# Pre-norms issued per token tile inside the part before, and first products by token tile, in a two-model transformer kernel on one core

## The chip, the cores and the metric

The kernel runs as one program on one core of a Trainium2 chip. The metric is the device time of one execution in microseconds (us); lower is better. A profiled execution gives, besides its time, a span (from the first to the last instruction) and a record of every instruction on the engines: TensorE (PE; PEld is its weight load), VectorE (DVE), ScalarE (ACT), GpSimd (POOL) and SyncE (SP), which issues the transfers.

## The reference

Two blocks run one behind the other on 256 tokens of width 1024, in float32. Every part is "add the normed output to the residual stream", and every part begins with a norm of that stream (the pre-norm).

```python
# first block
f = swiglu(rmsnorm(h, ffn1_pre_g)); h = h + 0.5 * rmsnorm(f, ffn1_post_g)
z = rmsnorm(h, mix_pre_g) @ w_in          # attention heads and a bidirectional RWKV-7 recurrence
h = h + rmsnorm(concat(y_att, y_rwkv) @ w_out, mix_post_g)
f = swiglu(rmsnorm(h, ffn2_pre_g)); h = h + 0.5 * rmsnorm(f, ffn2_post_g)
# second block, two layers; hc is a second stream of 256 context tokens
hx = rmsnorm(h, norm1_g) * (1 + scale) + shift   # shift, scale from a modulation of c
h = h + gate * mix(hx, hc)                # window attention and an mLSTM
h = h + gate * channel_mix(...)           # layer 0 a swiglu of 2816, layer 1 eight experts
```

swiglu(t) is (silu(t @ w_gate) * (t @ w_up)) @ w_down, with an inner width of 2816 (22 blocks of 128).

## The kernel before, in words

**Tiling.** The stream `hx` lies with tokens on the partitions, as two token tiles of 128 x 1024. A product needs the normed stream transposed (features on the partitions), so a pre-norm is: square with a sum on ScalarE (L184, in `rms_rstd`), `rstd` by two GpSimd instructions (L110, L111, in `rsqrt`), `xn` on VectorE (L217 with a gain row, L215 without), eight 128 x 128 transposes per tile on TensorE (L230 in `norm_rows_T`, L240 in `to_T`), and a split of the result in two float32r halves: `xhi` on ScalarE (L192, L200) and `xlo` on VectorE (L193, L201). Where a scale and a shift are columns (`ada_T`), VectorE applies them behind the transpose (L199).

**Products.** Every float32 product is three float32r products, hi*hi, hi*lo and lo*hi (`mm3`, L160 to L162). Weights are loaded in pieces of 1 MB into three raw buffers (L133) and split as they come, in tiles of 128 x 1024 elements: `whi` on ScalarE (L149), `wlo` on VectorE (L150). A phase has a number of split buffers (`nsplit`); phases lie one over the other in memory, so a buffer of a new phase waits for the last reader of what lay there.

**Parts.** `ffn_block` runs a feed-forward in two halves of 11 blocks of 128 inner features. For each pair of blocks `ffn` multiplies the weights by all 256 tokens, gate and up (192 products of 256 columns for the first four blocks), applies silu and the product (`hh`, already transposed as the down product needs it), and splits it (L276, L277). The down product goes by 512 output columns; the last 512 are done token tile by token tile (L288 to L296), and behind each tile `add_post` does the post-norm (L184, L327) and adds to `hx` (L328). `mix1` is the first mixer: pre-norm, one block of `rwkv_in` (L789), q, k and v of the attention (`mm_N`, token tile by token tile), the heads with the other blocks of `rwkv_in` between them, the recurrence, and `w_out` (L797 to L810), where four accumulators (two tiles, two halves of columns) fill together. `mix2` is the mixer of the second block; its first products take the context tiles first.

**Order.** The program is traced in the order written; the build's scheduler then sets the order on each engine's queue, taking what is ready in its own estimate, earlier-written work first. Each engine then works its queue in that order. Pre-norms stand at the beginning of their part: `norm_rows_T` at L333 and L786, `ada_T` at L881.

Of the kernel before, what the change touches and what calls it, by code (L numbers as in the profile page):

```python
# [9 lines left out]
F32 = mybir.dt.float32  # L10
# [23 lines left out]
class Builder:  # L34
# [185 lines left out]
    def norm_rows_T(self, pool, h, name, bufs=1, tags=("ps",)):  # L220

        x = self.new_xT()
        xn = self.norm_N(h, self.row(pool, name, bufs))
        for t in range(2):
            ts = slice(t * 128, (t + 1) * 128)
            for k0 in range(0, KT, 4):
                p = self.psum(4, 128, tag=tags[(2 * t + k0 // 4) % len(tags)])
                for k in range(4):
                    c = (k0 + k) * 128
                    self.nc.tensor.transpose(p[:, k], xn[t][:, c:c + 128], self.ident)  # L230
                self.split_t((x[0][:, k0:k0 + 4, ts], x[1][:, k0:k0 + 4, ts]), p)
        return x

    def to_T(self, xn, dst, k0, n, g=None, b=None, tag="ps"):
        for kk in range(0, n, 2):
# [14 lines left out]
    def ffn(self, xs, wg, wu, wd, fp, nhalf=2):  # L250
# [3 lines left out]
        for hf in range(nhalf):  # L254
            hhi = fp.tile([128, per, ng * S], F32R, name="hhi")
            hlo = fp.tile([128, per, ng * S], F32R, name="hlo")
            d0 = hf * per
            for blk in range(0, per, 2):
                nb = min(2, per - blk)
                c0 = (d0 + blk) * 128  # L260
                g = self.wsplit(kview(wg, 0, KT, c0, nb * 128), KT, nb * 128)
                u = self.wsplit(kview(wu, 0, KT, c0, nb * 128), KT, nb * 128)
                for j in range(nb):
                    cs = slice(j * 128, (j + 1) * 128)
                    for gi, x in enumerate(xs):
# [13 lines left out]
                yield None  # L279
# [50 lines left out]
    def ffn_block(self, h, pre, wg, wu, wd, post, early=None):  # L330
        nc = self.nc
        with self.phase("fp", 8, gu=2, ps=6) as fp:
            x = self.norm_rows_T(fp, h, pre, 2)  # L333
            if early:
                early()
            grow = self.row(fp, post, 2)
            y = self.row_tiles()
            for r in self.ffn([x], self.I[wg], self.I[wu], self.I[wd], fp):
                if r is not None:
                    hf, c, t, p = r  # L340
                    yv = y[t][:, c * 512:(c + 1) * 512]
                    if hf == 0:
                        nc.scalar.copy(yv, p)
                    else:
                        nc.vector.tensor_tensor(yv, p, yv, op=OP.add)
                        if c == 1:
                            self.add_post(h[:, t], y[t], grow, 0.5)
                yield

# [428 lines left out]
    def mix1(self, side):  # L778
        nc = self.nc
        I = self.I  # L780
        with self.phase("ra") as ra:
            rkv = ra.tile([128, 12, S], F32, name="rkv")
            R = (rkv,) + tuple(ra.tile([128, S], F32, name=n) for n in ("wd", "ad", "gd"))
            R += (ra.tile([128, 4, 2, 2], F32, name="rn"), self.load_const(ra, "k_blk", nc.sync))
            with self.phase("ap", 4, acc=2, rn=1, **{"as": 2}, at=1, av=1, ps=1) as mp:
                x = self.norm_rows_T(mp, self.hx, "mix_pre_g", 1, ("as", "at", "av", "ps"))  # L786
                yT = self.new_xT()
                win = self.rwkv_in(mp, x, R)
                next(win)  # L789
                yield from self.attn1(mp, x, yT, win)  # L790
                yield from win
            with self.phase("rp", None, c0=2, c1=2, c2=2, md=2) as mp:
# [4 lines left out]
                with self.phase("wo", 4) as me:  # L797
                    y = self.row_tiles()
                    grow = self.row(me, "mix_post_g")
                    accs = [[self.psum(512, tag=g) for _ in range(2)] for g in ("md", "c2")]  # L800
                    for kb in range(0, KT, 2):
                        for c in range(2):
                            w = self.wsplit(kview(I["w_out"], kb * 128, 2, c * 512, 512), 2, 512)
                            for t, x, ts in self.tiles((0, yT)):
                                for k in range(kb, kb + 2):
                                    self.mm3(accs[c][t], (x[0][:, k, ts], x[1][:, k, ts]), w(k - kb), k == 0, k == KT - 1)
                    for t in range(2):
                        for c in range(2):
                            nc.scalar.copy(y[t][:, c * 512:c * 512 + 512], accs[c][t])
                        self.add_post(self.hx[:, t], y[t], grow)  # L810
                        yield

# [58 lines left out]
    def mix2(self, L, side, pre=None):  # L871
# [1 line left out]
        w = self.I["w_in_2"][L]  # L873
        both = L == 0
        with self.phase("m2", 4, acc=2, ps=1, at=3, ml=2) as mp:
            if pre is None:
                x = self.ada_T(self.hx, L, 0, 0)
                c = self.ada_T(self.hc, L, 0, 1)
            else:
                c = pre  # L880
                x = self.ada_T(self.hx, L, 0, 0)  # L881
# [30 lines left out]
            first = cx + xx if pre else xx + cx  # L912

            def c_kv(col, n, t, p):
                nc.vector.tensor_tensor(gt[:, t], p[:, 256:272], bg, op=OP.add)
# [571 lines left out]
        yield  # L1487


class Halves:  # L1490


# [141 lines left out]
def program(tc, I, out):  # L1634
    b = Builder(tc, I)
    b.out = out
    with ExitStack() as ctx:
        b.open_pools(ctx)
        b.consts()
        b.cond()  # L1640
        run(b.ffn_block(b.hx, "ffn1_pre_g", "ffn1_w_gate", "ffn1_w_up", "ffn1_w_down", "ffn1_post_g"))
        side = b.mod(0)
        run(b.mix1(side))
        run(side)
        pre = []

        def early():
            b.load_ctx()
            pre.append(b.ada_T(b.hc, 0, 0, 1))

        run(b.ffn_block(b.hx, "ffn2_pre_g", "ffn2_w_gate", "ffn2_w_up", "ffn2_w_down", "ffn2_post_g", early))
# [42 lines left out]
```

## Time and profile before

| | us |
|---|---|
| median of 3 runs | 2451.85 (2451.59 to 2456.05) |
| the profiled execution | 2451.68 |
| its span | 2449.9 |
| TensorE busy | 2346.6 (96%) |
| first feed-forward, about | 0 to 203 |
| first mixer, about | 203 to 538 |
| second feed-forward, about | 538 to 743 |
| second block, about | 743 to 2450 |

The page gives shares for the whole span; the four borders between parts are a small share of it and have to be looked at one by one, by the waits of TensorE, by windows of time, and by the timeline. The granted clock of TensorE has two levels here, 1.00 (2.4 GHz) and 0.50 (1.2 GHz); a mean in between is a stretch with both.

### The profile page before, as it was taken

The page shows a single profiled execution, that of the slowest core. Times are in us where ns is not written, and L with a number is a line of the kernel's source. Part 1 is how long each engine was busy: PE and PEld are TensorE (multiplying, and loading weights), DVE is VectorE, ACT ScalarE, POOL GpSimd, SP SyncE. Part 2 cuts the span into 40 slices and gives each one's busy share as a digit, 9 for nine tenths or more (in the row PEclk, how much of TensorE's full clock was granted, in tenths as well). Part 3 has the DMA queues.
Part 4 walks back from the last instruction along what each step waited for, and adds up shares of the span by engine and source line. Part 5 has one row for each costly group of instructions (what it writes and reads, how often), then busy time and mean ns, then how long its engine had stood idle before and what let it go on. Part 6 is the DMA issues. An engine that isn't in the chain of part 4 may idle for free. (4 is left out here: it accounts for less than half of the span.)

```text
span 2449.9 us, 38791 instructions
## 1 busy us (share of the span) xinstructions
PE 2346.6 (96%) x15592; PEld 1963.8 (80%) x15592; DVE 1614.4 (66%) x2427; ACT 1307.0 (53%) x2038; POOL 188.2 (8%) x248
## 2 busy tenths in 40 slices
PE   7998989979998999999999999989999999999996
PEld 7996866659998767799899886778888887788875
DVE  5555667656547466443333464669989989889897
ACT  5543644345545355433223243567887777777764
POOL 0001112110001000200100110020100110020000
PEclk9999999999999999999999999999999999999998
DMA  8654342275652350232322235469999999999993
GB/s 261 198 187 138 122 162 88 81 237 170 202 173 88 102 172 21 70 118 82 110 93 82 83 113 175 135 237 373 335 352 341 343 345 335 352 339 335 365 343 134
DMA packets 281100, 489.56 MB, mean 200 GB/s; under 512 B 11424, under 2 KB 116896, under 8 KB 280912
## 3 DMA queue, kind: packets, MB, share of 16 engines
q1 hardware_dynamic: 280832, 486.80, 58.2%
q8 instruction: 124, 2.03, 0.3%
q14 instruction: 64, 0.52, 0.1%
q0 software_dynamic: 80, 0.21, 0.0%
HBM read 485.92 MB, written 1.05 MB: 199 GB/s over the span
## 5 line engine op out<-in xcount | busy, mean ns | idle before, releaser
L150 DVE TENSOR_TENSOR wlo<-wraw,whi 128x1024 fp32r<-128x1024 f32 (+1 forms) x830 | 975.5, 1208 | 227.9 <-ACT whi L149 221.9
L149 ACT CAST whi<-wraw 128x1024 fp32r<-128x1024 f32 (+1 forms) x832 | 824.6, 1030 | 257.9 <-PE ps L162 102.2
L161 PE MATMUL gu<-xlo,whi 128*128 128x256 f32 x1408 | 394.4, 280 | 4.0 <-DVE xlo L193 2.4
L160 PE MATMUL gu<-xhi,whi 128*128 128x256 f32 x1408 | 394.6, 281 | 0.8 <-ACT xhi L200 0.8
L162 PE MATMUL gu<-xhi,wlo 128*128 128x256 f32 x1408 | 393.8, 280 | 0.0
L161 PE MATMUL gu<-wlo,X 128*128 128x512 f32 (+1 forms) x768 | 291.2, 379 | 4.4 <-DVE wlo L150 3.4
L162 PE MATMUL gu<-whi,X 128*128 128x512 f32 (+1 forms) x768 | 286.2, 373 | 0.0
L160 PE MATMUL gu<-whi,X 128*128 128x512 f32 (+1 forms) x768 | 285.1, 374 | 0.0
L161 PEld LDWEIGHTS gu<-xlo,whi 128*128 128x128 f32 x1408 | 264.8, 188 | 5.3 <-DVE xlo L193 2.9
L160 PEld LDWEIGHTS gu<-xhi,whi 128*128 128x128 f32 x1408 | 264.7, 188 | 2.2 <-ACT xhi L200 1.4
L162 PEld LDWEIGHTS gu<-xhi,wlo 128*128 128x128 f32 x1408 | 265.2, 188 | 0.0
L161 PEld LDWEIGHTS gu<-wlo,X 128*128 128x128 f32 x768 | 144.7, 188 | 45.5 <-DVE wlo L150 21.3
L160 PEld LDWEIGHTS gu<-whi,X 128*128 128x128 f32 x768 | 144.7, 188 | 25.5
L162 PEld LDWEIGHTS gu<-whi,X 128*128 128x128 f32 x768 | 144.7, 188 | 23.6
L274 DVE TENSOR_TENSOR hh<-sg,gu 128x256 f32<-128x256 f32 x88 | 36.8, 418 | 164.6 <-ACT sg L272 164.6
L161 PE MATMUL acc<-wlo,xhi 128*128 128x512 f32 (+1 forms) x368 | 141.8, 386 | 3.1 <-DVE wlo L150 3.1
L160 PE MATMUL acc<-whi,xhi 128*128 128x512 f32 (+1 forms) x368 | 140.8, 385 | 2.5 <-ACT whi L149 1.1
L162 PE MATMUL acc<-whi,xlo 128*128 128x512 f32 (+1 forms) x368 | 141.6, 385 | 0.1
L161 PE MATMUL dn<-wlo,hT 128*128 128x512 f32 x352 | 140.6, 399 | 0.0
L162 PE MATMUL dn<-whi,hT 128*128 128x512 f32 x352 | 138.6, 394 | 0.0
L160 PE MATMUL ps<-whi,hhi 128*128 128x512 f32 x352 | 137.2, 390 | 0.0
L162 PE MATMUL ps<-whi,hlo 128*128 128x512 f32 x352 | 137.1, 390 | 0.0
(461 smaller groups left out, 3740.7 us busy)
## 6 DMA issues: line engine op xcount, KB each, us to landing
wraw<-in_exp_w_dram SPq DMA_DIRECT2D x235, 1024.0 KB, 7.0
wraw<-in_w_mod_dram SPq DMA_DIRECT2D x48, 1024.0 KB, 5.2
wraw<-in_w_in_dram SPq DMA_DIRECT2D x29, 1024.0 KB, 5.2
wraw<-in_exp_w_dram SPq DMA_DIRECT2D x58, 512.0 KB, 6.7
wraw<-in_ffn_w_dram SPq DMA_DIRECT2D x28, 1024.0 KB, 5.3
wraw<-in_ffn_w_gate_dram SPq DMA_DIRECT2D x20, 1024.0 KB, 5.7
wraw<-in_ffn_w_up_dram SPq DMA_DIRECT2D x20, 1024.0 KB, 5.5
wraw<-in_ffn_w_down_dram SPq DMA_DIRECT2D x16, 1024.0 KB, 5.1
```

What stands on the lines that cost most here:

```text
L149: nc.scalar.copy(hi, raw[:, k0:k0 + n])
L150: eng.tensor_tensor(lo, raw[:, k0:k0 + n], hi.bitcast(F32), op=OP.subtract)
L160: mm(out, l[0], r[0], start=start, stop=False)
L161: mm(out, l[0], r[1], start=False, stop=False)
L162: mm(out, l[1], r[0], start=False, stop=stop)
L274: nc.vector.tensor_tensor(hh, sg, pg[:, 1], op=OP.mult)
```

## The change

A new class `Ahead` holds a pre-norm that is issued in steps: `norm(t)` for one token tile (square, `rstd`, `xn`, and a row of shifts if there is one) and `turn(t)` (eight transposes and the split). The pre-norm of the first mixer is issued by tile inside the end of the first feed-forward, that of the second feed-forward inside the end of `w_out`, that of the second block's first mixer inside the end of the second feed-forward (its scale and shift as rows, made by 16 row products, in `ada_ahead`). In each, `norm(0)` stands behind tile 0's `add_post`, `turn(0)` ahead of tile 1's `add_post`, `norm(1)` and `turn(1)` behind it. The first four blocks of a feed-forward are multiplied token tile by token tile, tokens stationary and weights moving, so `hh` comes out with tokens on the partitions and is transposed back. `w_out` does columns 0 to 511 for both tiles, then 512 to 1023 tile by tile. `mix1` has seven split buffers in place of four and no block of `rwkv_in` ahead of the attention.

```diff
@@ in ffn, per half @@
-            for blk in range(0, per, 2):
+            if hf == 0 and ng == 1:
+                x = xs[0]
+                ws = [[self.wsplit(kview(w, 0, KT, blk * 128, 256), KT, 256) for w in (wg, wu)] for blk in (0, 2)]
+                for t in range(2):
+                    ts = slice(t * 128, (t + 1) * 128)
+                    for bi, blk in enumerate((0, 2)):
+                        pg = self.psum(2, 256, tag="gu")
+                        for m in range(2):
+                            for k in range(KT):
+                                self.mm3(pg[:, m], (x[0][:, k, ts], x[1][:, k, ts]), ws[bi][m](k), k == 0, k == KT - 1)
...
+                        tp = self.psum(2, 128)
+                        for j in range(2):
+                            nc.tensor.transpose(tp[:, j], hh[:, j * 128:(j + 1) * 128], self.ident)
+                        self.split_t((hhi[:, blk:blk + 2, ts], hlo[:, blk:blk + 2, ts]), tp)
+                    yield None
+            for blk in range(4 if hf == 0 and ng == 1 else 0, per, 2):
@@ in ffn_block @@
-            x = self.norm_rows_T(fp, h, pre, 2)
-            if early:
-                early()
+            if isinstance(x, str):
+                a = self.ahead(h, self.row(fp, x, 2))
+                for t in range(2):
+                    a.norm(t)
+                    a.turn(t)
+                x = a.x
             grow = self.row(fp, post, 2)
+            a = nxt(fp)
...
                         if c == 1:
+                            if t == 1:
+                                a.turn(0)
                             self.add_post(h[:, t], y[t], grow, 0.5)
+                            a.norm(t)
+                            if t == 1:
+                                a.turn(1)
@@ in mix1 @@
-            with self.phase("ap", 4, acc=2, rn=1, **{"as": 2}, at=1, av=1, ps=1) as mp:
-                x = self.norm_rows_T(mp, self.hx, "mix_pre_g", 1, ("as", "at", "av", "ps"))
+            with self.phase("ap", 7, acc=2, rn=1, **{"as": 2}, at=1, av=1, ps=1) as mp:
+                x = self.x
...
-                next(win)
...
+                    a = self.ahead(self.hx, self.row(me, "ffn2_pre_g", tag="grow2"), None, ("c0", "c1"))
...
+                    accs = [self.psum(512, tag="md") for _ in range(2)]
                     for kb in range(0, KT, 2):
+                        w = wo(kb, 0)
+                        for t in range(2):
+                            part(accs[t], t, kb, w)
                     for t in range(2):
+                        nc.scalar.copy(y[t][:, 0:512], accs[t])
+                    ws = [wo(kb, 1) for kb in range(0, KT, 2)]
+                    for t in range(2):
+                        acc = self.psum(512, tag="c2")
+                        for i in range(4):
+                            part(acc, t, 2 * i, ws[i])
+                        nc.scalar.copy(y[t][:, 512:], acc)
+                        if t == 1:
+                            a.turn(0)
                         self.add_post(self.hx[:, t], y[t], grow)
+                        a.norm(t)
                         yield
+                    a.turn(1)
@@ new, beside ada_T @@
+    def ada_ahead(self, pool, h, L, n, gi):
+        rows = []
+        for i, src in enumerate((self.gsT[:, L, n], self.modT[:, L, 24 * n:24 * n + 8])):
+            g = pool.tile([128, D], F32, name="arow%d" % i, tag="arow%d" % i)
+            for c, p in enumerate(self.row_psum(lambda k: src[:, k, gi:gi + 1])):
+                self.nc.scalar.copy(g[:, c * 512:(c + 1) * 512], p.rearrange("p a b -> p (a b)"))
+            rows.append(g)
+        return self.ahead(h, *rows)
@@ in mix2 @@
+            x = self.x or self.ada_T(self.hx, L, 0, 0)
@@ new class @@
+class Ahead:
...
+    def norm(self, t):
+        nc = self.b.nc
+        xn = self.xn[t] = self.b.sm.tile([128, D], F32, name="xn", bufs=2)
+        rstd = self.b.rms_rstd(self.h[:, t], xn)
+        nc.vector.scalar_tensor_tensor(xn, self.h[:, t], rstd, self.grow, op0=OP.mult, op1=OP.mult)
+        if self.brow is not None:
+            nc.vector.tensor_tensor(xn, xn, self.brow, op=OP.add)
+
+    def turn(self, t):
...
+        for k0 in range(0, KT, 4):
+            p = b.psum(4, 128, tag=self.tags[self.n % len(self.tags)])
+            self.n += 1
+            for k in range(4):
+                b.nc.tensor.transpose(p[:, k], self.xn[t][:, (k0 + k) * 128:(k0 + k + 1) * 128], b.ident)
+            b.split_t((x[0][:, k0:k0 + 4, ts], x[1][:, k0:k0 + 4, ts]), p)
@@ in program @@
+        run(b.ffn_block(b.hx, "ffn1_pre_g", "ffn1_w_gate", "ffn1_w_up", "ffn1_w_down", "ffn1_post_g",
+                        lambda p: b.ahead(b.hx, b.row(p, "mix_pre_g", 2))))
...
+        def nxt(p):
             b.load_ctx()
             pre.append(b.ada_T(b.hc, 0, 0, 1))
+            return b.ada_ahead(p, b.hx, 0, 0, 0)
+        run(b.ffn_block(b.hx, b.x, "ffn2_w_gate", "ffn2_w_up", "ffn2_w_down", "ffn2_post_g", nxt))
```

## Rows read from the trace of the kernel before

**Rows 1.** The page, busy time by engine: us, share, instructions.

```profile
PE 2346.6 (96%) x15592; PEld 1963.8 (80%) x15592; DVE 1614.4 (66%) x2427; ACT 1307.0 (53%) x2038; POOL 188.2 (8%) x248
```

**Rows 2.** Waits of TensorE, whole run: us in total, times, longest.

```profile
PE ps L230 <- DVE xn L217: 24.1, 2, 13.7
PE as L230 <- DVE xn L217: 9.1, 1, 9.1
PE ps L240 <- DVE xn L215: 8.7, 3, 5.8
```

**Rows 3.** Windows: length, busy us (PE, PEld, DVE, ACT, POOL), clock, DMA share, GB/s.

```profile
203.20:212.30 9.10, 0.00 (x1) 0.00 (x1) 6.82 (x8) 7.10 (x10) 5.83 (x8) 0.61 0.37 125
212.30:218.00 5.70, 5.64 (x25) 4.61 (x25) 5.31 (x7) 2.35 (x4) 0.35 (x1) 0.73 0.89 297
...
537.90:548.20 10.30, 0.00 (x0) 0.00 (x0) 8.47 (x7) 8.39 (x14) 6.98 (x8) 0.75 0.07 27
548.20:560.20 12.00, 10.52 (x48) 9.79 (x48) 9.95 (x15) 8.42 (x14) 2.29 (x5) 0.50 0.58 174
560.20:575.00 14.80, 14.80 (x128) 14.80 (x126) 14.50 (x24) 8.68 (x15) 0.00 (x0) 1.00 0.55 170
743.00:751.00 8.00, 0.93 (x3) 0.61 (x3) 5.07 (x6) 5.30 (x9) 5.37 (x8) 0.80 0.02 2
...
515.00:537.80 22.80, 21.87 (x95) 17.21 (x93) 9.32 (x11) 9.36 (x12) 1.62 (x2) 1.00 0.89 286
```

**Rows 4.** TensorE's timeline at 978 us, row products: start, us, what.

```profile
978.32 1.95 PE L169 MATMUL ml<-k_ident,modT 128*128 128x128 f32 x16
980.02 0.48 PE L160 MATMUL acc<-whi,xhi 128*128 128x512 f32 x1
```

**Rows 5.** Timeline behind the first feed-forward: start, us, what, [idle before, releaser].

```profile
203.20 0.69 DVE L345 TENSOR_TENSOR xn<-ps,xn 128x512 f32<-128x512 f32 x1 [2.04 <-PE ps L162]
206.08 1.28 DVE L327 SCALAR_TENSOR_TENSOR xn<-xn,rstd,grow 128x1024 f32<-128x1024 f32 x1 [2.19 <-POOL rstd L111]
...
212.69 1.28 DVE L217 SCALAR_TENSOR_TENSOR xn<-hx,rstd,grow 128x1024 f32<-128x1024 f32 x1 [0.44 <-POOL rstd L111]
...
206.08 1.98 ACT L149 CAST whi<-wraw 128x1024 fp32r<-128x1024 f32 x2
...
212.30 1.12 PE L230 MATMUL as<-k_ident,xn 128*128 128x128 f32 x4 [9.14 <-DVE xn L217]
```

**Rows 6.** VectorE's groups, 203.2 to 218.6 us: busy us, mean ns, idle before.

```profile
L150 DVE TENSOR_TENSOR wlo<-wraw,whi 128x1024 fp32r<-128x1024 f32 x4 | 4.9, 1215 | 0.0
...
L328 DVE TENSOR_TENSOR hx<-xn,hx 128x1024 f32<-128x1024 f32 x1 | 1.2, 1224 | 0.0
...
L193 DVE TENSOR_TENSOR xlo<-as,xhi 128x512 fp32r<-128x512 f32 x1 | 0.7, 680 | 0.0
```

**Rows 7.** VectorE's groups, 541 to 575 us.

```profile
L199 DVE TENSOR_SCALAR sp_t<-ps,gsT,modT 128x256 f32<-128x256 f32 x8 | 4.0, 536 | 1.1 <-PE ps L240 1.1
L201 DVE TENSOR_TENSOR xlo<-sp_t,xhi 128x256 fp32r<-128x256 f32 x8 | 3.3, 421 | 0.1
...
L215 DVE TENSOR_SCALAR xn<-hc,rstd 128x1024 f32<-128x1024 f32 x2 | 1.5, 746 | 0.4 <-POOL rstd L111 0.4
```

**Rows 8.** TensorE's timeline in the second block's first mixer.

```profile
763.42 0.40 PE L160 MATMUL acc<-whi,xhi 128*128 128x272 f32 x1 [0.62 <-ACT xhi L200]
```

**Rows 9.** Timeline at the start, and transfers up to 30 us (KB, us to landing).

```profile
18.85 0.39 PE L161 MATMUL gu<-xlo,whi 128*128 128x256 f32 x1 [0.98 <-DVE xlo L193]
...
20.55 0.37 SPq L133 DMA_DIRECT2D wraw<-in_ffn_w_up_dram  x1
...
wraw<-in_ffn_w_up_dram SPq DMA_DIRECT2D x3, 1024.0 KB, 8.5
```

**Rows 10.** TensorE's timeline in the second feed-forward: first and last of seven products.

```profile
555.08 0.41 PE L162 MATMUL gu<-xhi,wlo 128*128 128x256 f32 x1
...
556.36 0.41 PE L162 MATMUL gu<-xhi,wlo 128*128 128x256 f32 x1
```

More of the change, by code (lines that the diff above doesn't have):

```diff
@@ L218, in norm_N, with ahead @@
         return xn
[L220 to L232, printed above, removed]
+    def ahead(self, h, grow, brow=None, tags=("ps",)):
+        return Ahead(self, h, grow, brow, tags)
     def to_T(self, xn, dst, k0, n, g=None, b=None, tag="ps"):
@@ L257, in ffn @@
             d0 = hf * per
-            for blk in range(0, per, 2):
+            if hf == 0 and ng == 1:
[8 more added lines that the diff above has]
+                                self.mm3(pg[:, m], (x[0][:, k, ts], x[1][:, k, ts]), ws[bi][m](k), k == 0, k == KT - 1)
+                        sg = fp.tile([128, S], F32, name="sg", bufs=2)
+                        nc.scalar.activation(sg, pg[:, 0], AF.Silu)
+                        hh = fp.tile([128, S], F32, name="hh", bufs=2)
+                        nc.vector.tensor_tensor(hh, sg, pg[:, 1], op=OP.mult)
+                        tp = self.psum(2, 128)
[4 more added lines that the diff above has]
+            for blk in range(4 if hf == 0 and ng == 1 else 0, per, 2):
                 nb = min(2, per - blk)
@@ L328, in add_post, with ffn_block @@
         nc.vector.tensor_tensor(h, y, h, op=OP.add)
-    def ffn_block(self, h, pre, wg, wu, wd, post, early=None):
+    def ffn_block(self, h, x, wg, wu, wd, post, nxt):
         nc = self.nc
         with self.phase("fp", 8, gu=2, ps=6) as fp:
-            x = self.norm_rows_T(fp, h, pre, 2)
-            if early:
-                early()
+            if isinstance(x, str):
[4 more added lines that the diff above has]
+                x = a.x
             grow = self.row(fp, post, 2)
+            a = nxt(fp)
             y = self.row_tiles()
@@ L799, in mix1, with part @@
                     grow = self.row(me, "mix_post_g")
-                    accs = [[self.psum(512, tag=g) for _ in range(2)] for g in ("md", "c2")]
-                    for kb in range(0, KT, 2):
[L802 to L806, printed above, removed]
-                    for t in range(2):
-                        for c in range(2):
-                            nc.scalar.copy(y[t][:, c * 512:c * 512 + 512], accs[c][t])
+                    a = self.ahead(self.hx, self.row(me, "ffn2_pre_g", tag="grow2"), None, ("c0", "c1"))
+                    wo = lambda kb, c: self.wsplit(kview(I["w_out"], kb * 128, 2, c * 512, 512), 2, 512)
+                    def part(acc, t, kb, w):
+                        ts = slice(t * 128, t * 128 + 128)
+                        for k in range(kb, kb + 2):
+                            self.mm3(acc, (yT[0][:, k, ts], yT[1][:, k, ts]), w(k - kb), k == 0, k == KT - 1)
+                    accs = [self.psum(512, tag="md") for _ in range(2)]
+                    for kb in range(0, KT, 2):
+                        w = wo(kb, 0)
+                        for t in range(2):
+                            part(accs[t], t, kb, w)
+                    for t in range(2):
+                        nc.scalar.copy(y[t][:, 0:512], accs[t])
[7 more added lines that the diff above has]
+                            a.turn(0)
                         self.add_post(self.hx[:, t], y[t], grow)
+                        a.norm(t)
                         yield
+                    a.turn(1)
+            self.x = a.x
     def load_ctx(self):
@@ L875, in mix2 @@
         with self.phase("m2", 4, acc=2, ps=1, at=3, ml=2) as mp:
[L876 to L881, printed above, removed]
+            c = pre
+            x = self.x or self.ada_T(self.hx, L, 0, 0)
+            self.x = None
             rt = self.load_const(mp, "k_rope2", nc.sync)
@@ L911, in mix2 @@
             cx, xx = self.tiles((2, c)), self.tiles((0, x))
-            first = cx + xx if pre else xx + cx
+            first = cx + xx
             def c_kv(col, n, t, p):
@@ L1487, in expert, with __init__ @@
         yield
+class Ahead:
+    def __init__(self, b, h, grow, brow, tags):
+        self.b, self.h, self.grow, self.brow, self.tags = b, h, grow, brow, tags
+        self.x, self.xn, self.n = None, {}, 0
+    def norm(self, t):
[6 more added lines that the diff above has]
+    def turn(self, t):
+        b = self.b
+        if self.x is None:
+            self.x = b.new_xT()
+        x, ts = self.x, slice(t * 128, (t + 1) * 128)
+        for k0 in range(0, KT, 4):
[4 more added lines that the diff above has]
+            b.split_t((x[0][:, k0:k0 + 4, ts], x[1][:, k0:k0 + 4, ts]), p)
 class Halves:
@@ L1640, in program @@
         b.cond()
-        run(b.ffn_block(b.hx, "ffn1_pre_g", "ffn1_w_gate", "ffn1_w_up", "ffn1_w_down", "ffn1_post_g"))
+        run(b.ffn_block(b.hx, "ffn1_pre_g", "ffn1_w_gate", "ffn1_w_up", "ffn1_w_down", "ffn1_post_g",
+                        lambda p: b.ahead(b.hx, b.row(p, "mix_pre_g", 2))))
         side = b.mod(0)
```

3 lines of the change are left out of this document (1 added, 2 removed).

## The prediction

> **What bounds the kernel now.** I read the page's busy line first: TensorE is busy for 96% of the span, 2346.6 of 2449.9 us [rows 1]. So only about 103 us can be won by filling its idle time, and what adds work to it is paid nearly in full. The waits of TensorE then say where those 103 us lie [rows 2]: in transposes of a normed input that wait for VectorE's `xn`. Two waits on L217 under `ps` sum to 24.1 us, the longest 13.7 (the start of the program), so the other is 10.4 (`w_out` to the second feed-forward); 9.1 us under `as` lies between the first feed-forward and the first mixer; the longest of three L240 waits, 5.8 us, opens the second mixer. The change touches these four places. The windows show what a place costs beyond its wait [rows 3]: between 203.2 and 212.3 us TensorE does nothing, and the clock granted it is 0.61 there and 0.73 until 218; between 537.9 and 548.2 nothing again, then 48 instructions in 12.0 us at 0.50, the 1.2 GHz level, before it runs 128 instructions in 14.8 us, 0.116 each.
>
> Set against useful work at full rate (row products and transposes 0.106 us: 16 from 978.32 to 980.02 [rows 4]; 512-wide products 0.23 us: 95 in 21.87 [rows 3]), 203.2 to 218 holds 16 transposes and 9 products, 3.8 us of work in 14.8: **11.0 us lost**. 537.9 to 560.2 holds 32 transposes and 16 products, 5.3 us in 22.3: **17.0 us lost**. Those two are the prize.
>
> **Why the wait is there.** Behind the first feed-forward the timeline is the chain of the second token tile [rows 5]: last sum into `y` at 203.20, post-norm L327 at 206.08 (2.9 us for the square on ScalarE and `rstd` on GpSimd), its add behind it to 208.6, then the pre-norm's square and `rstd`, and `xn` at 212.69. Tile 0's `hx` was done 33 x 0.23 = 7.6 us earlier, at 201.0, because its last 33 products ran ahead of tile 1's. Its pre-norm had only to be issued there.
>
> **The change, part by part.** The sum is against the profiled execution, 2451.68 us (span 2449.9 and 1.8 around it), 0.17 below the median of the three runs.
>
> *First feed-forward to first mixer.* Tile 0: `hx` at 201.0, square, `rstd` and `xn` in 2.2 + 1.28 us [rows 5], L345 of tile 1 (0.69) in between, so `xn` ends near 205.2 and its 8 transposes start there, not at 212.30. Tile 1's own chain stays. What is late next is VectorE, which works in order: from 203.2 it owes L345 0.69, two `xn` and one L327 at 1.28 each, L328 1.22, four `xlo` at 0.68 and the four low halves of the q weights at 1.22 [rows 5, 6], together 13.3 us: 216.5. No weight of the mixer is cast before 206.08 [rows 5]: its split buffers are laid over `hhi` and `hlo`, which the last products read, and seven in place of four don't free them sooner. So tile 0's 24 q products end at 216.5 plus 1.4 for the last six, 218, where before 9 were done: 15 x 0.23 = **3.4 us** won. Bounds: 0, if the build's scheduler keeps tile 1's chain ahead, and 9.1, the whole wait.
>
> *`w_out` to the second feed-forward.* Columns 512 to 1023 now go tile by tile, the same 96 products in all. Tile 0 ends 24 x 0.23 = 5.5 us before 537.8, at 532.3. Copy, square, `rstd`, L327 and L328 take 5.3 us and the pre-norm 3.4, by the same rows: `xn` of tile 0 at 541.0. From there VectorE owes L327 and L328 2.5, `xn` of tile 1 1.3, four `xlo` 2.7, the eight low halves that tile 0's 96 products need 9.7, and the context's two `xn` 1.5 [rows 5 to 7]: 17.7 us, to 558.7. If the context's eight L199 and eight L201, 7.6 us more [rows 7], go behind the weights, tile 0's products end at 558.7 + 1.4 = 560, 96 done where there were 16: 80 x 0.116 = 9.3 us. If they go in between, it is 567. TensorE then starts at 546.6 (L327, L328, two `xlo`, one low half behind 541) and has had 20.4 us, of which I take 2.7 for a low clock until about 552 and 3.4 for 32 transposes: 14.3 us, 123 products, against 16 + 58 before: 5.7 us. I take the middle, **7.5 us**; bounds 0 and 11 (of the 17, what is left behind a chain that takes to 541 and a split).
>
> *Second feed-forward to second mixer.* Context products come first there, before and after; they wait for the low halves of their weights, and those for VectorE. On it the new form costs two `xn` and two shift adds (5.0) and four `xlo` (2.7), where eight L199 and L201 and two L215 stood (9.1); half of the new work falls into its idle time, 2.9 of 8.0 us before 751 [rows 3]. Won: eight transposes in TensorE's idle time, 0.9 us, and the 0.62 us wait for `xhi` at 763.42 [rows 8], less half a low half of delay: **1.0 us**; bounds -2 and 5.8, the wait [rows 2].
>
> *Start.* Tile 0's first products need nothing of tile 1, but they use up a split twice as fast: 12 products, 1.4 us, per low half of 1.22 us, with four `xlo` and two `xn` on the same engine. I take **0**; bounds 1.5 won (from 18.85, when the last `xlo` is there [rows 9], back to tile 0's) and 3 lost (the fourth weight late, rival 4).
>
> *Added on TensorE.* Each feed-forward turns eight blocks of `hh` back, 16; the scale and shift rows of the second mixer take 16 row products. 32 x 0.106 = **3.4 us** [rows 4]; bounds 0 (all in idle time) and 7.0 (at 0.22, as the 16 from 212.30 to 215.8 ran). The 192 products of the first two blocks stay 192 of 256 columns.
>
> *At nothing:* the three row loads moved to earlier places in SP's queue (0.5 MB each, ahead of weight loads that wait for buffers; uncovered, at most half of the 8.5 us of a 1 MB load each [rows 9]); the first block of `rwkv_in` (48 products), no longer ahead of q, k and v, taken up by TensorE's idle time among the attention heads, and uncovered 5.5 us; four copies of rows on ScalarE inside the feed-forward.
>
> Sum: -3.4 - 7.5 - 1.0 + 0 + 3.4 = -8.5. **2451.7 - 8.5 = 2443.2 us.** Behind each place TensorE runs without a gap, so what is won there stays won.
>
> **Rivals.**
> 1. *The wait is filled whole:* splits get in ahead of the norms, and tile 0's products cover tile 1's chain. -8 - 11 - 3 and 2 for added work: -20, 2431.7. For it: VectorE idles 2.3 of 9.1 us before 212.3 and 1.8 of 10.3 before 548.2 [rows 3]. Against: that is little, and the casts start late.
> 2. *VectorE is the bound:* reordering on a full engine only moves the idle time, or the scheduler keeps the old order, so that the change doesn't do what it says. Half of each gain, added work in full: -1.7 - 3.8 - 0.5 + 3.4 = -2.6, 2449.1. For it: VectorE is busy 5.31 of 5.70 us up to 218 and 9.95 of 12.0 up to 560.2 [rows 3].
> 3. *The clock stays low through tile 0.* After `w_out` 16 transposes, 16 products and 16 more transposes left it at 0.50 until 560 [rows 3], a product taking 0.213 us (six from 555.08 to 556.36 [rows 10]). If tile 0's 96 run so from 546.6, they take 20.4 us, to 567 and not 560: 7 us gone, 2450.2. Against it: behind the first feed-forward mostly transposes preceded the return to 1.00, which a mean of 0.73 puts before 218 [rows 3]. The Trainium skill (TensorE: Matmul & The Clock Gate, Part 4) says that transposes don't count as busy for the clock. By that rule tile 0's transposes in the gap would not hold the clock up, and this rival would come true: 2450.2. The first boundary speaks against the rule, the second for it.
> 4. *Slower: tile 0 starves.* A split that feeds one tile lasts 1.4 us (12 products of 256 columns, six of 512), and VectorE makes one in 1.22 us only if it does nothing else. Place: the first splits at the start, at q and after `w_out`. At the start the fourth weight is asked for at 20.55, lands 8.5 us later [rows 9], its low halves end near 32; TensorE, running from 18.85, would want it after 72 products, at 27.2, and could fill some with tile 1: 3 us lost. If the same eats the other gains, 3 + 3.4 = +6.4, 2458.1. It decides from where tile 0's first 96 products take over 15 us at the start.
>
> **Chances.** Forecast 0.47; rival 1 0.15; rival 2 0.14; rival 3 0.10; rival 4 0.14. A measurement here tells about 0.2%, 4.9 us, from no change: below 2446.9 is faster, forecast and rival 1, 0.62; rivals 2 and 3 lie within, 0.24; rival 4 is slower, 0.14. The range 2433 to 2456 leaves out most of rival 4 and half of rival 1.
>
> **What would show it.** Right: among TensorE's waits the 9.1 and 10.4 us shrink to about 2 and 3, with shorter waits on `wlo` or `xlo` behind them; the first transposes start near 205 and 541 on the old scale of time; VectorE has no gap for 13 us behind each boundary. Wrong: tile 0's transposes behind tile 1's L328 (rival 2); product spacing of 0.213 for over 10 us after `w_out` (rival 3); waits of `gu` on `wlo` of several us at the start (rival 4); a new wait of TensorE among the attention heads or in the recurrence, which I hold unchanged.

## The result, and the profile after

The changed kernel is slower: 2477.52 us (median of 4) against 2452.39 (4 runs beside it), a ratio of 1.0101, 95% interval 1.0089 to 1.0113. I had forecast 2443.2. The page, against [rows 1]:

```profile
span 2475.1 us, 38887 instructions
...
PE 2360.5 (95%) x15640; PEld 1974.8 (80%) x15640; DVE 1613.9 (65%) x2417; ACT 1307.8 (53%) x2038; POOL 179.8 (7%) x248
```

The span is 25.2 us longer, TensorE's busy time 13.9; so part of the loss is waiting, part the 48 added instructions and the same work at a lower clock. TensorE's waits, against [rows 2] (the new class's transposes are L1557, its `xn` L1544, its shift row L1546):

```profile
PE ps L1557 <- DVE xn L1544: 23.8, 3, 13.7
PE ps L1557 <- DVE xn L1546: 12.7, 2, 9.9
PE c L1557 <- DVE xn L1544: 9.1, 2, 5.9
...
PE gu L161 <- DVE wlo L150: 6.0, 15, 1.3
```

No wait for `xn` has gone. The start's 13.7 is there, and each border now has two: one for each token tile. To place the loss I read from TensorE's timeline where each part's first and last product start. Stretches of the profiled execution before, and what each is longer in a kernel, in us (letters: the experiments below; the two stretches from a feed-forward's first down product to its last, 121.9 us each in every kernel, are left out):

| | start to first down product | border 1: first feed-forward to first mixer product | that to end of `rwkv_in` | recurrence, to first `w_out` product | `w_out` | border 2: to first down product | border 3 and second mixer | rest |
|---|---|---|---|---|---|---|---|---|
| before | 80.9 | 13.0 | 105.0 | 191.4 | 25.2 | 83.2 | 289.1 | 1418.2 |
| after | +5.4 | +1.7 | +4.0 | +3.3 | +0.4 | +4.2 | +7.3 | -1.0 |
| a | +1.4 | +1.7 | +4.3 | +2.3 | +0.4 | +3.7 | +4.4 | +3.0 |
| b | +6.2 | -2.7 | +13.9 | +3.4 | +1.0 | +4.1 | +5.5 | +1.4 |
| c | +5.5 | -2.7 | +15.8 | +2.3 | +0.5 | +5.2 | +4.2 | +0.1 |
| d | +1.8 | +0.2 | +3.7 | +2.5 | +1.6 | +3.0 | +4.2 | +1.0 |
| e | +5.4 | +1.7 | +2.1 | +3.5 | +0.2 | +3.5 | +7.3 | -1.2 |
| f | +5.4 | +1.7 | +4.1 | +3.3 | +0.4 | +0.4 | +0.6 | +0.9 |
| g | +2.0 | 0.0 | 0.0 | +2.3 | +0.4 | -1.2 | +1.0 | -0.5 |
| h | +1.3 | 0.0 | 0.0 | +0.2 | -0.1 | -2.3 | +0.9 | +0.5 |
| i | +3.3 | +3.4 | +3.9 | +1.5 | -0.1 | +5.0 | +6.0 | -0.4 |
| j | 0.0 | -7.4 | +8.4 | +1.9 | -0.1 | -4.7 | +6.4 | +1.4 |
| k | +1.8 | -7.4 | +7.2 | +0.9 | -0.1 | -2.4 | +0.9 | +1.0 |
| l | +0.2 | 0.0 | 0.0 | +0.8 | -0.2 | -4.8 | +0.6 | -0.6 |
| m | +1.7 | -7.4 | +7.6 | 0.0 | -0.2 | -4.4 | +0.5 | +0.6 |
| p | 0.0 | -7.4 | +7.6 | +0.4 | -0.1 | -1.5 | +6.9 | +0.9 |

Each row is one execution. Its noise can be read off stretches whose code is the same as before: 2.0 at the start (g; k and m alike), 2.4 at border 2 (k), 6.9 in the second mixer (p; j alike; both at the end of this document). Parts are therefore judged by repeated runs, and the table says where to look.

**Border 2, TensorE.** Timeline behind the last `w_out` product of the changed kernel:

```profile
552.23 0.40 PE L162 MATMUL c<-whi,xlo 128*128 128x512 f32 x1
555.83 1.94 PE L1557 MATMUL c<-k_ident,xn 128*128 128x128 f32 x8 [3.20 <-DVE xn L1544]
563.71 1.97 PE L1557 MATMUL c<-k_ident,xn 128*128 128x128 f32 x8 [5.94 <-DVE xn L1544]
568.05 1.29 PE L230 MATMUL ps<-k_ident,xn 128*128 128x128 f32 x4 [2.37 <-DVE xlo L193]
...
572.12 2.13 PE L169 MATMUL ps<-k_ident,gsT 128*128 128x128 f32 x14
574.09 1.95 PE L169 MATMUL ps<-k_ident,modT 128*128 128x128 f32 x16
575.79 0.37 PE L160 MATMUL gu<-whi,xhi 128*128 128x256 f32 x1
```

`w_out` ends 14.8 us later than before, so tile 0's transposes stand at 541.0 on the old scale, as forecast. Then TensorE waits for tile 1, turns it, turns the context, makes 32 row products, and only then takes tile 0's first product: 561.0 on the old scale, where I had 546.6. Everything that is written ahead of that product stands ahead of it in the queue; its weights' low halves, the last part of their split, come earlier:

```profile
565.04 2.35 DVE L150 TENSOR_TENSOR wlo<-wraw,whi 128x1024 fp32r<-128x1024 f32 x2
```

The late first product is not in itself the 4.2 us lost there. The whole stretch, from the last `w_out` product to the first down product, before and after:

```profile
537.45:620.70 83.25, 71.42 (x563) 70.29 (x562) 58.45 (x78) 49.40 (x77) 9.28 (x12) 0.90 0.51 161
552.23:639.65 87.42, 75.01 (x603) 73.05 (x601) 56.25 (x77) 50.53 (x79) 5.02 (x10) 0.90 0.48 149
```

TensorE's idle time is 11.8 us before and 12.4 after, its busy time 3.6 us more for 40 more instructions (32 row products and eight transposes of `hh`). So the order won nothing, and the loss is nearly all added work.

**Border 1, ScalarE.** Its timeline behind the first feed-forward (last product at 208.17):

```profile
206.59 1.06 ACT L184 ACTIVATE xn<-hx 128x1024 f32<-128x1024 f32 x1 [3.59 <-DVE hx L338]
...
210.72 1.07 ACT L192 CAST xhi<-ps 128x512 fp32r<-128x512 f32 x2 [2.98 <-PE ps L1557]
211.67 1.07 ACT L184 ACTIVATE junk<-xn 128x1024 bf16<-128x1024 f32 x1
...
216.36 1.06 ACT L184 ACTIVATE xn<-hx 128x1024 f32<-128x1024 f32 x1 [3.52 <-DVE hx L338]
...
217.41 1.97 ACT L149 CAST whi<-wraw 128x1024 fp32r<-128x1024 f32 x2
```

The first cast of a mixer weight stands behind both of tile 1's squares, 9.2 us behind the last product; before, it filled the hole between them, 3.3 us behind (206.08 [rows 5] and 202.77, the last product's start). ScalarE idles 3.5 us in that hole, with the first three weight loads issued from 180.99 on and no transfer running any more (0 GB/s from 205 to 216.4).

**The start, SP's queue.**

```profile
2.85 2.52 SPq L133 DMA_DIRECT2D wraw<-in_ffn_w_up_dram  x1
14.83 0.34 SPq L177 DMA_DIRECT2D grow<-in_mix_pre_g_dram  x1
15.21 0.43 SPq L133 DMA_DIRECT2D wraw<-in_ffn_w_gate_dram  x1
20.55 0.37 SPq L133 DMA_DIRECT2D wraw<-in_ffn_w_up_dram  x1
```

The load of the first mixer's gain row waits for its buffer, whose first holder is the row that the start's own `xn` reads, and the third weight waits behind it: asked for at 15.21, where the kernel before asked at 5.43.

**Windows** (columns as in [rows 3]): the start; border 1 up to tile 1's transposes and from there; border 2 in the same two halves; border 3.

```profile
13.60:34.50 20.90, 17.27 (x115) 16.37 (x116) 13.70 (x16) 10.48 (x14) 0.00 (x0) 0.92 0.87 268
208.40:219.80 11.40, 1.27 (x10) 0.87 (x9) 7.04 (x8) 5.15 (x8) 1.80 (x7) 0.77 0.21 63
219.80:228.20 8.40, 7.21 (x20) 5.68 (x21) 8.19 (x10) 5.67 (x7) 0.00 (x0) 0.50 0.75 233
552.50:563.70 11.20, 2.07 (x9) 1.54 (x8) 6.28 (x6) 7.24 (x13) 3.73 (x7) 0.65 0.01 5
563.70:575.80 12.10, 9.72 (x57) 9.02 (x57) 10.85 (x15) 9.45 (x15) 1.29 (x4) 0.62 0.44 129
766.60:776.60 10.00, 0.06 (x2) 0.01 (x1) 6.31 (x7) 4.77 (x7) 3.96 (x7) 0.50 0.18 55
```

Border 1 after its transposes runs at 0.50 for 8.4 us, where the kernel before averaged 0.73 over 5.7 [rows 3]. VectorE, which I had named as the next bound, is busy 7.04 of 11.40 and 6.28 of 11.20 us.

### The profile page after: what moved, and what is told of

It reads as the page before. It is cut to its first block, busy times and chain, and to the rows that moved or that the text cites. A ratio compares the mean times of both kernels' runs of the same rounds, so it can differ in the third digit from the quotient of the medians.

```text
span 2475.1 us, 38887 instructions
## 1 busy us (share of the span) xinstructions
PE 2360.5 (95%) x15640; PEld 1974.8 (80%) x15640; DVE 1613.9 (65%) x2417; ACT 1307.8 (53%) x2038; POOL 179.8 (7%) x248
## 5 line engine op out<-in xcount | busy, mean ns | idle before, releaser
L160 PE MATMUL gu<-xhi,whi 128*128 128x256 f32 x1280 | 358.8, 281 | 0.8 <-ACT xhi L200 0.8
L161 PE MATMUL gu<-xlo,whi 128*128 128x256 f32 x1280 | 357.6, 280 | 1.7 <-DVE xlo L201 1.5
L162 PE MATMUL gu<-xhi,wlo 128*128 128x256 f32 x1280 | 357.2, 279 | 0.0
L160 PEld LDWEIGHTS gu<-xhi,whi 128*128 128x128 f32 x1280 | 240.3, 188 | 1.5 <-ACT xhi L200 1.4
L161 PEld LDWEIGHTS gu<-xlo,whi 128*128 128x128 f32 x1280 | 239.6, 187 | 2.4 <-DVE xlo L201 2.3
L162 PEld LDWEIGHTS gu<-xhi,wlo 128*128 128x128 f32 x1280 | 240.8, 188 | 0.0
```

The costliest lines, as they stand in the source:

```text
L160: mm(out, l[0], r[0], start=start, stop=False)
L161: mm(out, l[0], r[1], start=False, stop=False)
L162: mm(out, l[1], r[0], start=False, stop=stop)
```

## The experiments

Theory **Q**: engines work their queues in order, and what the change writes earlier blocks what it was to feed. Theory **S**: the first products by token tile starve on the splits (rival 4). Medians are given with the ratio to the kernel before.

**a.** Only the preparation for the part after next moves behind the first products.

```diff
-            a = nxt(fp)
-            y = self.row_tiles()
-            for r in self.ffn(...):
+            a = None
+            for i, r in enumerate(self.ffn(...)):
+                if i == 1:
+                    a = nxt(fp)
+                    y = self.row_tiles()
```

> Only the preparation of the part after next (row load of the first mixer's gain; context load, its norm and 16 transposes, 32 row products for scale and shift) is written behind the first four blocks of each feed-forward, not ahead of them. Theory Q (queues work in order, and what is written earlier stands earlier): at the start the third weight load no longer stands behind a row load that waits for its buffer, 3 to 5 of the 5.4 us lost there come back; behind w_out the first gate product no longer stands behind 48 transposes and row products, 3 to 5 us. Sum -6 to -10: 2467 to 2471. Theory S (the first products by token tile use up the splits faster than VectorE makes them): the waits turn into waits on wlo, 0 to -3: 2474 to 2478.

Measured 2472.04, 1.0077 (1.006 to 1.0094): 5.5 us less than the change, 1 us short of what Q gave. The start gives back 4.0, as Q has it; border 2 only 0.5: the first product comes 7.7 us earlier there, but the wait of 5.94 for tile 1's transposes stays in front, and the work that was moved is done later.

**b.** Only tile 1's transposes are written elsewhere: behind tile 0's first products (not at border 2).

```diff
-                for t in range(2):
-                    a.norm(t)
-                    a.turn(t)
+                a.norm(0)
+                a.turn(0)
+                a.norm(1)
...
+                for i, r in enumerate(self.attn1(mp, x, yT, win)):
+                    if i == 0:
+                        self.x.turn(1)
```

> Only tile 1's transposes are moved: written behind tile 0's first products at the start, behind tile 0's q products in the first mixer, behind the two context products in the second. Behind w_out they stay. Theory Q: in the second mixer the 9.9 us wait for tile 1's xn is filled with context products as before the change, -6 to -9; in the first mixer q of tile 0 need not wait for tile 1, but its split weights stand behind tile 1's squares on ScalarE, -1 to -2; start 0 to -1. Sum -7 to -12: 2465 to 2470. Theory S: the wait moves to wlo, 0 to -4: 2473 to 2478.

Measured 2482.74, 1.0123: slower than the change, against both theories. TensorE's timeline:

```profile
219.33 0.79 PE L160 MATMUL acc<-whi,xhi 128*128 128x512 f32 x1 [7.38 <-ACT whi L149]
...
232.27 1.09 PE L405 MATMUL ps<-k_ident,a_r 128*128 128x128 f32 x4 [3.27 <-DVE a_r L398]
234.03 1.12 PE L1565 MATMUL ps<-k_ident,xn 128*128 128x128 f32 x4 [0.68 <-ACT a_QT L406]
```

The wait for `xn` has turned into one of 7.4 us for the weights' casts, still behind tile 1's squares. And I put the transposes behind the place where tile 0's q is read: they now stand behind its rotary chain. That place costs part of the 13.9 us in the table; with it put right, and the row elsewhere, k below has 7.2. At border 3 the build's order kept four of the transposes ahead of the context products:

```profile
783.49 1.12 PE L1565 MATMUL ps<-k_ident,xn 128*128 128x128 f32 x4 [9.95 <-DVE xn L1554]
```

So b does not test the place there; border 3 gives back 1.8 of 7.3.

**c.** Both, and at border 2 too.

> Both moves, and tile 1's transposes of the second feed-forward behind tile 0's first products as well. Theory Q: the two sums and 2 to 4 us more behind w_out, -15 to -24: 2453 to 2462. Theory S: not under 2470.

Measured 2482.52, 1.0124, some 20 us over what Q gave. As b at border 1; at border 2 the first product comes 12.3 us earlier, the first down product does not: TensorE now waits 5.7 and 2.3 us for the splits of its weights.

**d.** The change without first products by token tile.

```diff
-            if hf == 0 and ng == 1:
+            if 0:
```

> The change with the first four blocks of both feed-forwards multiplied as before the change (all 256 tokens at once, nothing transposed back); everything else of the change stays. Theory Q: the products were behind tile 1's transposes anyway, so little is lost or won: 16 transposes fewer, -1 to -3: 2474 to 2477. Theory S: the starvation at the start and in the second feed-forward goes, -6 to -11: 2466 to 2471.

Measured 2466.71, 1.0054: 10.8 less, as S has it. But see h. The profiled execution, the slowest of four, shows 7.2 of it: 3.6 at the start and 3.1 at border 3 and in the second mixer, the rest within what single executions differ by.

**e.** The change with the mixer's own order as before.

```diff
-            with self.phase("ap", 7, ...
+            with self.phase("ap", 4, ...
                 win = self.rwkv_in(mp, x, R)
+                next(win)
```

> The change with the first mixer's own order as before: one block of rwkv_in ahead of q, k and v again, four split buffers again. The pre-norm stays ahead. In the changed kernel 4.0 us are lost between the first q product and the end of rwkv_in. Theory Q (place in the queue: the 48 products of that block were the cover of the attention's stalls): 3 to 4 us come back, 2473 to 2475. Rival C (the 4.0 us are the low clock behind the boundary, which stays 0.50 until the engine has run for some time whatever stands first): 0 to 1, 2476 to 2478.

Measured 2474.12, 1.0091: 3.4 less, as Q has it; the stretch after q gets 1.9 of its 4.0 back. The rest fits the low clock, which no run separates: from the first q product of the changed kernel, at 222.95, it is 0.50 to 228.2, and half of those 5.3 us is 2.6.

**f.** The change with border 3 as before.

```diff
...
-            return b.ada_ahead(p, b.hx, 0, 0, 0)
```

> The change with the second block's first mixer normed as before (no rows of scale and shift, no norm ahead; its transposes again in the mixer, between the context products). In the changed kernel 7.2 us are lost from the last product of the second feed-forward to the first product of the next part. Theory Q (context products no longer cover the norm, since tile 1's transposes are written ahead of them): all of that comes back and 1 to 3 us for the 32 row products that stand ahead of the second feed-forward, -8 to -10: 2467 to 2470. Rival C (it is the clock): -2 to -4.

Measured 2467.59, 1.0059: 9.9 less, the upper end of what Q gave: 6.7 at border 3 and 3.8 at border 2, where the 32 row products are gone. TensorE at border 3 in the changed kernel:

```profile
776.59 1.97 PE L1557 MATMUL ps<-k_ident,xn 128*128 128x128 f32 x8 [9.95 <-DVE xn L1546]
779.59 0.60 PE L160 MATMUL acc<-whi,xhi 128*128 128x272 f32 x1 [1.04 <-DVE xlo L193]
```

Context products, which need nothing of tile 1, wait behind it. But their weights are late too:

```profile
772.95 2.08 ACT L149 CAST whi<-wraw 128x1088 fp32r<-128x1088 f32 x2
```

```profile
776.45 2.49 DVE L150 TENSOR_TENSOR wlo<-wraw,whi 128x1088 fp32r<-128x1088 f32 x2
```

The first high half is cast 11.4 us behind the last product, behind tile 1's second square; in the kernel before, 3.3 us behind:

```profile
745.89 2.08 ACT L149 CAST whi<-wraw 128x1088 fp32r<-128x1088 f32 x2
```

How the 6.7 us divide between the place of the transposes and the late splits no run shows.

**g.** The kernel before with `w_out` by token tile and the norm ahead at border 2, nothing else.

> The kernel before with the w_out part of the change alone: columns 512 to 1023 token tile by token tile, the pre-norm of the second feed-forward ahead by tile; its first products by 256 tokens as before. My term of the prediction for this place was 7.5 us won, with first products by tile. Theory Q: products of 256 tokens need tile 1's transposes, which end when they did before, so 0 to 1 won there, and 2 lost at the start of w_out, whose weights are split later: 2452 to 2455 where before is 2452.5. Rival P (the prediction): the transposes of tile 0 and the context leave the path, 2 to 5 won, 2447 to 2450.

Measured 2454.17 (11 runs), 1.0006 (0.9997 to 1.0015). Nothing won, as Q has it.

**h.** The kernel before with first products by token tile, nothing else.

> The kernel before with the first four blocks of both feed-forwards by token tile alone (16 transposes of hh with it). Theory S (starvation): 1 to 3 us lost at the start, 2 to 4 in the second feed-forward: 2455 to 2460. Theory Q: the loss at the start was the row load ahead of a weight load, which this kernel does not have: 0 to 2 lost in all, 2452 to 2455.

Measured 2452.92 (11 runs), 1.0001 (0.9992 to 1.001). Alone, this part costs nothing in the total. With a, d and i it places the start, if that is read by TensorE's clock, which rises at 16.6 to 18.5 us in some executions and at 22.5 to 23.8 in others (the same code in both groups: last section). Early rise: neither part 0 (the kernel before, j, l, p), products by tile alone +1.3 and +1.4 (h, a), with the blocked load +5.4 (after; e and f alike). Late rise: neither +1.7 to +2.0 (g, k, m), the blocked load alone +1.8 (d), products by tile alone +3.3 (i). So by tile costs 1.4, the blocked load nothing, both together 5.4: by tile, the first 96 products ask for all four weights, and the third was asked for 10 us later. (In the change the clock also falls again from 30.2 to 33.7, some 1.7 of the 5.4. Late rise too: b 6.2 and c 5.5, where tile 1's transposes move as well; c has no blocked load, so that move costs about 2 us itself.)

**i.** The change with the two gain rows in memory that outlives both parts.

```diff
+            self.rows = self.res.tile([128, 2, D], F32, name="rows", tag="hc", bufs=1)
...
-                        lambda p: b.ahead(b.hx, b.row(p, "mix_pre_g", 2))
+                        lambda p: b.ahead(b.hx, b.pre_row(0, "mix_pre_g"))
```

> The change with one edit: the gain rows of the two pre-norms issued ahead (first mixer, second feed-forward) lie in the place that the context stream takes later, not in a buffer of the phase that ends. Theory P (a phase's buffers are handed on only when its last reader is placed: the row kept the old phase open until tile 1's xn, so every split of the next weights stands behind tile 1's squares on ScalarE, first cast 9.0 us after the last product behind the first feed-forward where before it was 2.9): casts move in front of tile 1's second square, 2 to 4 us at each of the two borders, and the row load no longer waits at the start, 4: 2465 to 2470. Rival Q (only the order in which the steps are written counts): the start alone, 2471 to 2474.

Measured 2473.86, 1.0086, the time that Q gave. ScalarE's timeline at border 1:

```profile
209.56 1.07 ACT L192 ACTIVATE junk<-xn 128x1024 bf16<-128x1024 f32 x1
...
210.61 1.99 ACT L149 CAST whi<-wraw 128x1024 fp32r<-128x1024 f32 x2
214.25 1.06 ACT L192 ACTIVATE xn<-hx 128x1024 f32<-128x1024 f32 x1 [1.65 <-DVE hx L346]
```

Half of theory P is shown: with the row outside the ending phase the casts stand in the hole again; and `w_out`'s first product waits 0.29 us for its high half, as before the change, where it waits 2.24 in the change and in g. Its gain at border 1 didn't come: the products stay behind tile 1's transposes, whose `xn` the splits now delay.

**j, k, l.** So both are needed. From the kernel before: rows in outliving memory, `turn(1)` behind tile 0's products and ahead of what reads them, the context behind the first products; k at border 1, l at border 2, j at both.

```diff
@@ mm_N @@
+                if mid:
+                    mid()
+                    mid = None
                 consume(blk[0][0], n, t, acc)
@@ mix1 @@
+                yield from self.attn1(mp, x, yT, win, lambda: late.turn(1))
@@ ffn_block @@
+                if i == 0:
+                    if bt:
+                        pre.turn(1)
...
+                if i == 2 and early:
+                    early()
```

> The kernel before with the borders behind the first feed-forward and behind w_out rebuilt: rows in the context's place, tile 1's transposes written behind tile 0's first products and ahead of what reads those, first products of the second feed-forward by token tile, the context's norm behind them, rwkv_in behind q, k and v. Second mixer and start as before. Theory P+Q: tile 0's products fill part of the wait for tile 1, 3 to 5 us won behind the first feed-forward, 4 to 7 behind w_out, 2 lost in the attention: 2441 to 2448. Rival V (VectorE and the low clock are the bound there whatever the order): 2450 to 2455.

> The same rebuilt border behind the first feed-forward alone; all else as before. Theory P+Q: 3 to 5 won there, 2 lost in the attention, where the first block of rwkv_in no longer stands ahead: 2449 to 2452. Rival V: 2453 to 2456.

> The same rebuilt border behind w_out alone (w_out and the second feed-forward's first products by token tile, context behind them). Theory P+Q: 4 to 7 won: 2445 to 2449. Rival V: 2451 to 2455.

Measured (11 runs each): j 2448.53, 0.9987 (0.9978 to 0.9996); k 2452.27, 1.0000 (0.9991 to 1.0009); l 2449.20, 0.9990 (0.9981 to 0.9999). Border 2 wins 2.8 us, less than Q gave; border 1 nothing. j and k lie between their two theories, l 0.2 above P+Q's range. l, TensorE's timeline, two windows of [rows 3]'s kind and the whole stretch of border 2:

```profile
541.80 1.09 PE L1565 MATMUL c<-k_ident,xn 128*128 128x128 f32 x8 [3.19 <-DVE xn L1552]
544.57 0.58 PE L160 MATMUL gu<-whi,xhi 128*128 128x256 f32 x1 [1.67 <-ACT whi L149]
547.27 0.58 PE L161 MATMUL gu<-wlo,xhi 128*128 128x256 f32 x1 [2.13 <-DVE wlo L150]
...
561.31 1.04 PE L1565 MATMUL ps<-k_ident,xn 128*128 128x128 f32 x8
```

```profile
537.90:548.20 10.30, 3.31 (x17) 2.29 (x16) 7.44 (x8) 8.47 (x13) 2.51 (x5) 0.78 0.19 63
548.20:560.20 12.00, 11.91 (x95) 11.71 (x94) 9.62 (x11) 7.21 (x11) 1.50 (x4) 0.90 0.92 310
538.21:616.68 78.47, 69.66 (x570) 67.71 (x569) 55.89 (x78) 48.77 (x75) 4.75 (x10) 0.96 0.56 187
```

Where the kernel before ran nothing and then 48 instructions at 0.50 [rows 3], l runs 17 and 95, and tile 1's transposes wait for nothing. In the whole stretch TensorE idles 8.8 us, 3.0 less than before.

**m, p.** Does border 1 lack the `rwkv_in` block as cover? j and k with that block behind tile 0's q products (and seven split buffers).

```diff
+                for i, r in enumerate(self.attn1(mp, x, yT, win, lambda: late.turn(1))):
+                    if i == 0:
+                        next(win)
+                    yield
```

> Both rebuilt borders (as in j_all_rebuilt), and the first block of rwkv_in written behind tile 0's q products, where before the change it stood ahead of q; seven split buffers in the first mixer, since four are all held by q there. Theory Q: that block covers the wait for the rest of the weights, and the attention loses nothing: 2 to 4 less than j_all_rebuilt, 2443 to 2447. Rival V (VectorE bounds the stretch, so the place of the block doesn't matter): 2448 to 2451.

> The rebuilt border behind the first feed-forward alone, with the first block of rwkv_in behind tile 0's q products. Theory Q: 2 to 4 less than k_mix1_rebuilt: 2448 to 2450. Rival V: as k_mix1_rebuilt, 2451 to 2454.

Measured (12 runs each): m 2451.97, 1.0001 (0.9992 to 1.0011); p 2453.80, 1.0011 (1.0002 to 1.002). Q falls here; V holds for p, and m lies 1 us above V's range. p is 2.2 us slower than the kernel before, its interval just clear of 1; but five of its twelve executions, the profiled one among them, lie at 2456.3 to 2459.2 with a mean granted clock of 0.982 to 0.984, and the profiled one lost its time in the second mixer (last section). So a loss at border 1 isn't shown either. p at border 1, ScalarE and VectorE:

```profile
206.24 1.07 ACT L192 ACTIVATE junk<-xn 128x1024 bf16<-128x1024 f32 x1
...
207.29 1.99 ACT L149 CAST whi<-wraw 128x1024 fp32r<-128x1024 f32 x2
```

```profile
209.66 1.23 DVE L339 TENSOR_TENSOR hx<-xn,hx 128x1024 f32<-128x1024 f32 x1
210.80 2.35 DVE L150 TENSOR_TENSOR wlo<-wraw,whi 128x1024 fp32r<-128x1024 f32 x2
```

The first high half starts behind tile 1's square and its first low half behind tile 1's post-norm. The high half lets one product start 7.4 us earlier, and the next waits for the low half, to 213.84 in m, whose feed-forward ends 1.7 us later than before: 3.7 us earlier than the first product at 215.8. Of that, the clock takes 1.7 (m, from 213.8 to 221.0):

```profile
213.80:221.00 7.20, 7.16 (x25) 5.76 (x26) 6.49 (x8) 4.82 (x6) 1.60 (x2) 0.76 0.74 234
```

and tile 1's eight transposes, no longer ahead of the first product, take 0.9. What is left, about 1 us, I did not place. That an earlier split would win there was not tried.

## Why the prediction was wrong

**The step that failed** is the same at all three borders: I took tile 0's products to run while tile 1's chain runs. "So tile 0's 24 q products end at 216.5 plus 1.4" and "TensorE then starts at 546.6" hold only if those products stand ahead of tile 1's transposes in TensorE's queue, and the splits of their weights ahead of tile 1's norm on ScalarE and VectorE. Neither was so. The diff writes `turn(1)`, the context's norm and the row products ahead of them, and my front text says that earlier-written work goes first. I applied that to the scheduler keeping the *old* order (rival 2), not to the new one. The splits were late: at borders 1 and 3 the first high half is cast 9.2 and 11.4 us behind the last product, where the kernel before has 3.3 at both; the forecast reckoned with the old 206.08. The Trainium skill (PSUM — Partial Sum Buffer, Engine vs sequencer instructions) says that matmuls start in program order and that ScalarE's and VectorE's queues are first in, first out; the trace agrees at border 2, where the first product's weights are split by 567.4 and it starts at 575.79, behind the context's transposes and the row products. No rival came near 2477.5: the only slower one, rival 4, gave 2458.1.

- *Border 1*, 3.4 won by forecast: 1.7 lost, and of the 4.0 behind it some 2 to 2.6 by the clock (an estimate, see e). The transposes of tile 0 came where I had them, 204.6 on the old scale. "What is late next is VectorE" was wrong in the change: it idled 4.4 of 11.4 us, the splits being queued behind tile 1's squares. The forecast's size was wrong too: rebuilt, the border wins 0 (k, p).
- *Border 2*, 7.5 won by forecast: nothing; the 4.2 lost are added work, and 3.3 more are lost ahead of `w_out`, of which g shows 2.3 alone. Tile 0's `xn` was right to 0.1 us. Rival 3's low clock did not meet tile 0's products either: it is back at 1.00 from 573.0. Rebuilt (l), 4.8 us of the stretch, of which as much as 2.4 can be the execution (k), and 2.8 of the time (0.2 to 4.7): the mechanism exists at about a third of its size.
- *Border 3*, 1.0 won by forecast: f gives back 9.9. "Context products come first there, before and after" failed: they stand behind both tiles' transposes, and their weights are split too late to go ahead of them.
- *Added work:* I counted 16 row products for the two rows; it is 16 for each, so 48 instructions, 5.1 us at 0.106, not 3.4; 40 of them lie at border 2.
- *At nothing:* wrong twice. The row load waits for a buffer, with a weight load behind it: with products by tile 4.0 us at the start (a). I had looked at what it moves, not at what it waits for. The first block of `rwkv_in`, uncovered 5.5, is worth 3.4 with the two edits of e.
- *Start*, 0 by forecast, 3 at worst: 5.4. Rival 4's place and sign were right there, but not its size, 3: products by tile alone cost 1.4 there and nothing in the total (h), and only together with the blocked load come to 5.4. The first 96 products took from 16.8 to 34.5, over its 15 us.

What each part is worth in the change, from the runs that undo it: a 5.5, d 10.8, e 3.4, f 9.9, in sum 29.6 for a loss of 25.1; a and d share the start.

## What to carry to other kernels

To overlap a chain with work that does not need it, write that work ahead of the chain's next blocking instruction on every queue, its weights' splits too, and look at what each moved load waits for as well as what it moves. Memory is part of the order: a row kept in an ending phase put the next phase's casts behind its last reader. And price a moved step with both tiles, since the stall of tile 1 remains after tile 0's is gone.

## What the runs showed that was not expected

In the profiled executions of j and p the second mixer, whose code is as before, is 6 to 7 us longer. The window of j and the same one of l:

```profile
866.00:881.00 15.00, 15.00 (x79) 9.02 (x78) 7.53 (x27) 5.78 (x19) 0.00 (x0) 0.87 0.59 199
```

```profile
866.00:881.00 15.00, 14.30 (x88) 8.33 (x86) 9.21 (x30) 6.25 (x19) 0.00 (x0) 1.00 0.44 144
```

The clock fell in one and not in the other, without a border near it. The start shows the same: one product of g, whose code is that of the kernel before up to `w_out`, lasts 0.41 us where the kernel before has 0.28 at the same time.

```profile
20.18 0.41 PE L160 MATMUL gu<-xhi,whi 128*128 128x256 f32 x1
```

```profile
20.02 0.28 PE L161 MATMUL gu<-xlo,whi 128*128 128x256 f32 x1
```

So gains of 2 or 3 us are seen only in the medians of many runs.
